# A fused two-layer transformer kernel: a new opening of the first phase (constant products ahead of the data, a first slab in two pieces on two queues, loads in order of use, squares of the rows later)

## The chip, the cores and the metric

The kernel runs on one core of one Trainium2 chip, as one program with one launch. The metric is the device time of that program in microseconds (us). The core has a matrix engine (TensorE, PE in the profile), whose weight loads are listed apart as PEld, a vector engine (DVE), a scalar engine (ACT), a general engine (POOL) and a queue engine (SP) that issues DMAs. Each engine works through a queue of its own in order, so an instruction that waits holds back all that stands behind it on that engine. Data comes from DRAM by DMA into the on-chip memory of 128 partitions; the matrix engine writes into eight accumulator banks of 128x512 numbers, which ACT and DVE empty.

## What is computed

Two transformer layers over 256 tokens of 2048 features. Layer 0 mixes tokens with two kinds of attention (block attention with 8 heads, and a compressed, selected and windowed attention with 8 heads in 2 groups), layer 1 with retention; each is followed by cross attention to a memory of 256 rows and a gated feed-forward net with a short convolution. All that the change touches lies at the start of layer 0:

```python
def _rmsnorm(x, g):
    y = xf * lax.rsqrt(jnp.mean(jnp.square(xf), axis=-1, keepdims=True) + RMS_EPS)
    return (y * g).astype(x.dtype)
...
hn = _rmsnorm(h, norm_mix[l])
mq, mk, mv, nq, nkc, nvc, nks, nvs, nkw, nvw, ng = _split(h @ w_in, AB_SIZES)
...
kc = _compress(k_c, pe_k, w1_k, w2_k)        # nkc -> compressed keys
vc = _compress(v_c, pe_v, w1_v, w2_v)        # nvc -> compressed values
p_c = softmax(q . kc);  o_c = p_c @ vc
o = gates[..., 0:1] * o_c + gates[..., 1:2] * o_s + gates[..., 2:3] * o_w
```

The first products of the kernel are nkc and nvc, 256 columns each, from columns 4096 to 4607 of `w_in_ab`. The kernel multiplies the weights with x times the gain first and applies the factor of the norm (one number per token, from the squares of the rows) to the results afterwards.

## The kernel before, in words

**Slabs and pieces.** The 2048 features are cut into 16 slabs of 128. A weight or an activation is kept as two parts, a high one (`hi`, an ACT copy to the rounded type fp32r) and a low one (`lo`, a DVE subtraction), and a product is the sum of three part products. `product_b_steps` (L258) makes 256 output columns with the weights as the stationary operand: per slab four matmuls of 512 columns (`upper`, L272: high weights on both parts of x) and four of 256 (`lower`, L277), counted over the two accumulators j of both first products. Every other step does `lower` first. `product_a_steps` (L295) makes columns with x as the stationary operand (L303 to L305). The two first products need all four accumulator pieces of the tag `acc` (L101); the product after them, columns 4864 to 5119, gets its two accumulators when those of the first of the two have been emptied by `halves` (L320): an ACT copy (L322), then a DVE addition (L324).

**The first phase (L359 to L409)** is written out by hand for ACT, DVE and PE (`manual_schedule`), so that their queues have the order of the code. It goes over 8 pairs of slabs p. For each pair SP issues the load of x (`load_x`) and of the two weight pieces (L388); ACT makes the high part of x (L197) and of the weights (L401), DVE the low parts (L200, L402); then each of the two products in `first` does one step. For pairs 0 to 3 the loads are pieces of 256 KB in order of use; then come all four remaining x loads, and weight loads of 512 KB for two pairs each. After pair 3, six tiny DVE memsets (L409) are placed on tiles which POOL's loads (constants, parameters, positions; L417, L421, L431, L453 and L128) fill later: POOL's loads wait for them.

**After the first phase** `layers()` (L1040) runs with only PE's order by hand; ACT, DVE, POOL and SP get theirs from the scheduler of the framework when the program is built. Beside the products stands a list of generators, `side`; `pump` (L244) advances the first two of them at each step of a product. Before the change the list is: `start_steps` (L619: loads of the rows, their squares on ACT by `norm.add`, L148, two steps after each load; then the norm's factors `col` and `row`; then, inside it, `angle_steps` for the rotary angles), `setup_steps`, and `compress` for k; `compress` for v is appended later. `compress` waits 8 steps, loads its weights and runs small matmuls (L687), ending for v with L723, which reads `hs` made by DVE at L716. `nsa_group` (L763) makes the scores against the compressed keys (L773), waits three steps and transposes the result (L803); DVE copies it to `pct` (L805). `nsa_head` (L808) then uses `pct` at L822, the first of the five matmuls that make a head's output.

Of the kernel before, what the change touches and what calls it, by code (L numbers as in the profile page):

```python
# [75 lines left out]
def hybrid_kernel(ctx: ExitStack, tc: tile.TileContext, a, out):  # L76
# [33 lines left out]

    ident = new([P, P])
    make_identity(nc, ident)
    ones = new([P, P])
    pool.memset(ones, 1.0)
# [143 lines left out]
    def product_b_steps(ws, xs, evac, step=4, n=None, turn=True):  # L258
# [4 lines left out]
        for i, k0 in enumerate(range(0, n, step)):  # L263
            ks = range(k0, min(k0 + step, n))
            parts = [next(ws) for _ in ks]
            last = ks[-1] == n - 1
            kj = [(k, j) for k in ks for j in range(2)]
            jk = [(k, j) for j in range(2) for k in ks]

            def upper(order, end):  # L270
                for k, j in order:
                    pe.matmul(acc[j], parts[k - k0][0][:, j * P : (j + 1) * P], xs[k], start=(k == 0),  # L272
                              stop=(end and k == n - 1))

            def lower(order, end):
                for k, j in order:
                    pe.matmul(acc[j][:, 0:S], parts[k - k0][1][:, j * P : (j + 1) * P], xs[k][:, 0:S], start=False,  # L277
                              stop=(end and k == n - 1))

            if turn and i % 2:  # L280
# [55 lines left out]
    def feed(norm, xs, gains):  # L336
# [12 lines left out]
        def f(g):  # L349
            for t in range(2):  # L350
# [9 lines left out]
    held = [[], []]  # L360
    ready = [deque(), deque()]
    first = [product_b_steps(iter(ready[i].popleft, None), xs_mix, lambda j, acc, i=i: held[i].append(halves(acc)),
                             step=2, n=ND) for i in range(2)]
    cst, cmask, tri_f, posi = new([P, 4]), new([P, 2, 16]), work((P, P)), new([P, S], I32, "w", 12)

    def load_x(p):

        nc.sync.dma_start(x_in[p].rearrange("p s t -> p (s t)"), a["x"][:, 2 * p * S : (2 * p + 2) * S])
# [5 lines left out]
    with tc.manual_schedule(engines=engines):  # L374
        act.activation(new([P, 1]), eps, AF.Copy, scale=eps)
        load_par(nc.sync, "mix")
        for p in range(ND // 2):
            i, c = p // 2, slice(p % 2 * 512, p % 2 * 512 + 512)
            if p % 2 == 0:
                raws = [raw_tile() for _ in range(2)]  # L380
                his = [new([P, 1024], F32R, "whi", 4) for _ in range(2)]
                los = [new([P, 1024], F32R, "wlo", 4) for _ in range(2)]
            if p < 4:
                load_x(p)
            for q in range(2):
                if p < 4 or p % 2 == 0:
                    d = c if p < 4 else slice(0, 1024)
                    nc.sync.dma_start(raws[q][:, d], w_ab.part(4 * i, 4, 4096 + 256 * q, 256)[:, d])  # L388
            if p == 3:
                for x in range(4, 8):  # L390
                    load_x(x)
            for s in (2 * p, 2 * p + 1):
                xs_mix.append(slab_tile())
                xhat_hi(xs_mix[s], x_in[p][:, s % 2, :], gain("mix")[:, s : s + 1])
            if p == 0:
                dve.tensor_copy(his[0][:, c], raws[0][:, c])
            for s in (2 * p, 2 * p + 1):
                xhat_lo(xs_mix[s], x_in[p][:, s % 2, :], gain("mix")[:, s : s + 1])
            for q in range(2):
                if p or q:  # L400
                    act.activation(his[q][:, c], raws[q][:, c], AF.Copy)  # L401
                dve.tensor_sub(los[q][:, c], raws[q][:, c], his[q][:, c].bitcast(F32))  # L402
# [3 lines left out]
            if p == 3:  # L406
# [205 lines left out]
    def mixer_ab(xs, row, col, kcv):  # L612
# [6 lines left out]
        def start_steps():  # L619
            norm = Norm()  # L620
            tg = [(t, g) for g in range(4) for t in range(2)]
            for i in range(10):
                if i < 8:
                    load_rows(*tg[i])
                if i > 1:
                    norm.add(*tg[i - 2])
                if i < 9:
                    yield
# [8 lines left out]
            yield from angle_steps(0, posi)  # L637
# [19 lines left out]
        def compress(i, kind, t, done):  # L657

            for _ in range(8):
# [79 lines left out]
        side.extend((start_steps(), setup_steps()))  # L739
# [23 lines left out]
        def nsa_group(g, qr, qu):  # L763
# [34 lines left out]
            yield  # L798
            yield
            yield  # L800
# [7 lines left out]
        def nsa_head(g, r, q):  # L808
# [9 lines left out]
            while len(comp) < 2:  # L818
# [389 lines left out]
```

## Time and profile before

| | before |
|---|---|
| time, median of 3 runs | 2839.22 us (2838.47 to 2839.59) |
| profiled execution, its own time | 2837.16 us |
| its span, first to last instruction | 2835.4 us (1.76 us lie around it) |
| PE busy | 2815.4 us (99%) |
| DVE busy | 1926.7 us (68%) |
| ACT busy | 1483.8 us (52%) |
| mean granted PE clock | 0.999 |

All engine times below are microseconds from the first instruction of the profiled execution. A timeline row has the start, the duration, the engine, the source line, the operation, output and inputs with their shapes, the count of merged instructions, and in brackets how long the engine had been idle before it and what released it. Matmuls overlap, and the end of one is modelled, so the pace of PE is read from start to start. A matmul between full float32 operands stands as two records in the trace.

### The profile page before, as it was taken

The numbers are of one execution on the slowest core, as the hardware profiler recorded it, in microseconds if no ns is written. First come the engines' busy times: TensorE is split into PE (matmuls) and PEld (weight loads), VectorE is DVE, ScalarE is ACT, GpSimd is POOL, SyncE is SP. The second block draws the span as 40 slices with busy tenths as digits, with TensorE's granted clock in tenths as the row PEclk, the third lists the DMA queues.
The fourth block names the chain that finished last, engine by engine and source line by source line (L and its number), as shares of the span: only waits on it lengthen the run. The fifth ranks groups of instructions, "written<-read, shape, count | busy, mean of one in ns | idle before, by whom it ended". The sixth has DMA issues, their size and how long they took to land.

```text
span 2835.4 us, 39564 instructions
## 1 busy us (share of the span) xinstructions
PE 2815.4 (99%) x14726; PEld 2404.8 (85%) x14726; DVE 1926.7 (68%) x3147; ACT 1483.8 (52%) x2193; POOL 29.9 (1%) x211
## 2 busy tenths in 40 slices
PE   8999999999999999999999999999999999999998
PEld 8888888888888888888888888888888888888887
DVE  7765766776767677665555555556777767676766
ACT  6444455664545555454444444444665645454554
POOL 0000000000000000000000000000000000000000
PEclk9999999999999999999999999999999999999999
DMA  9535564555555555555555555565545555555554
GB/s 320 163 120 162 182 209 170 173 191 193 186 193 188 191 193 203 191 185 179 179 179 178 193 178 179 183 206 190 186 168 189 189 191 191 191 188 193 192 188 155
DMA packets 150545, 530.12 MB, mean 187 GB/s; under 512 B 17040, under 2 KB 17456, under 8 KB 150352
## 3 DMA queue, kind: packets, MB, share of 16 engines
q1 hardware_dynamic: 148752, 523.65, 53.8%
q0 software_dynamic: 1024, 2.90, 0.4%
q8 instruction: 115, 1.88, 0.3%
q10 hardware_dynamic: 576, 1.05, 0.1%
q14 instruction: 78, 0.64, 0.1%
HBM read 525.43 MB, written 2.10 MB: 186 GB/s over the span
## 4 chain that ended last, share of the span: by engine, by line
PE 98%; DMA 1%; DVE 0%; ACT 0%; issue 0%; SPq 0%; ACTq 0%; DVEq 0%
PE acc L272 33%; PE acc L277 17%; PE acc L303 14%; PE acc L305 14%; PE acc L304 14%; PE bank L346 1%; PE bank L981 0%; DMA t<-in_w_in_ab_dram 0%; PE bank L499 0%; PE bank L491 0%; PE bank L479 0%; PE bank L1004 0%; PE bank L574 0%; PE bank L584 0%; PE bank L970 0%; PE bank L983 0%
## 5 line engine op out<-in xcount | busy, mean ns | idle before, releaser
L233 DVE TENSOR_TENSOR t<-t,t 128x1024 fp32r<-128x1024 f32 x954 | 1163.9, 1221 | 704.0 <-ACT t L232 701.1
L232 ACT ACTIVATE t<-t 128x1024 fp32r<-128x1024 f32 x954 | 1009.9, 1059 | 952.5 <-PE acc L305 564.2
L272 PE MATMUL acc<-t,t 128*128 128x512 f32 x4096 | 992.8, 392 | 6.6 <-DVE t L200 6.6
L272 PEld LDWEIGHTS acc<-t,t 128*128 128x128 f32 x4096 | 750.9, 189 | 151.6 <-DVE t L200 6.6
L303 PE MATMUL acc<-t,t 128*128 128x512 f32 (+2 forms) x1824 | 712.8, 391 | 2.6 <-DVE t L324 2.6
L305 PE MATMUL acc<-t,t 128*128 128x512 f32 (+2 forms) x1824 | 704.7, 386 | 0.0
L304 PE MATMUL acc<-t,t 128*128 128x512 f32 (+2 forms) x1824 | 704.1, 386 | 0.0
L277 PEld LDWEIGHTS acc<-t,t 128*128 128x128 f32 x4096 | 528.3, 191 | 22.2 <-issue 0.4
L277 PE MATMUL acc<-t,t 128*128 128x256 f32 x4096 | 539.4, 283 | 0.0
L303 PEld LDWEIGHTS acc<-t,t 128*128 128x128 f32 x1824 | 343.4, 188 | 72.4 <-DVE t L324 3.0
L304 PEld LDWEIGHTS acc<-t,t 128*128 128x128 f32 x1824 | 343.6, 188 | 69.0 <-issue 1.9
L305 PEld LDWEIGHTS acc<-t,t 128*128 128x128 f32 x1824 | 343.2, 188 | 69.3
L878 ACT ACTIVATE t<-acc 128x256 f32<-128x256 f32 x176 | 65.6, 373 | 151.1 <-PE acc L272 151.1
L881 DVE TENSOR_TENSOR t<-acc,t 128x256 f32<-128x256 f32 x176 | 74.1, 421 | 78.0 <-ACT t L878 77.8
L884 ACT ACTIVATE t<-t,t 128x256 f32<-128x256 f32 x176 | 104.6, 594 | 32.3 <-DVE t L882 32.0
L602 DVE TENSOR_TENSOR t<-t,acc 128x512 f32<-128x512 f32 x148 | 95.0, 680 | 2.1 <-PE acc L1099 2.1
L886 DVE SCALAR_TENSOR_TENSOR t<-t,t,t 128x256 f32<-128x256 f32 x176 | 84.5, 480 | 3.1
L885 DVE SCALAR_TENSOR_TENSOR t<-t,t,t 128x256 f32<-128x256 f32 x176 | 84.1, 478 | 0.7 <-ACT t L884 0.7
L882 DVE TENSOR_TENSOR t<-t,t 128x256 f32<-128x256 f32 x176 | 74.2, 422 | 3.0
L322 ACT ACTIVATE t<-acc 128x256 f32<-128x256 f32 x80 | 30.4, 382 | 67.0 <-PE acc L272 67.0
L324 DVE TENSOR_TENSOR t<-acc,t 128x256 f32<-128x256 f32 x80 | 33.4, 419 | 27.2 <-ACT t L322 27.0
L898 ACT ACTIVATE t<-t 128x256 f32<-128x256 f32 x88 | 36.0, 410 | 24.9 <-DVE t L886 24.9
(218 smaller groups left out, 1128.4 us busy)
## 6 DMA issues: line engine op xcount, KB each, us to landing
t<-in_w_up_dram SPq DMA_DIRECT2D x352, 512.0 KB, 3.3
t<-in_w_in_c_dram SPq DMA_DIRECT2D x192, 512.0 KB, 3.4
t<-in_w_down_dram SPq DMA_DIRECT2D x176, 512.0 KB, 3.3
t<-in_w_in_ab_dram SPq DMA_DIRECT2D x80, 512.0 KB, 3.6
t<-in_w_out_c_dram SPq DMA_DIRECT2D x64, 512.0 KB, 3.4
t<-in_w_out_ab_dram SPq DMA_DIRECT2D x32, 512.0 KB, 3.9
t<-in_w_kv_x_dram SPq DMA_DIRECT2D x32, 512.0 KB, 3.4
t<-in_w_q_x_dram SPq DMA_DIRECT2D x16, 512.0 KB, 3.2
```

The source lines that it names most:

```text
L232: act.activation(hi[:, 0 : m * ncol], raw[:, 0 : m * ncol], AF.Copy)
L233: dve.tensor_sub(lo[:, 0 : m * ncol], raw[:, 0 : m * ncol], hi[:, 0 : m * ncol].bitcast(F32))
L272: pe.matmul(acc[j], parts[k - k0][0][:, j * P : (j + 1) * P], xs[k], start=(k == 0), stop=(end and k == n - 1))
L277: pe.matmul(acc[j][:, 0:S], parts[k - k0][1][:, j * P : (j + 1) * P], xs[k][:, 0:S], start=False, stop=(end and k == n - 1))
L303: pe.matmul(o, xh, hi, start=(k == 0), stop=False)
L304: pe.matmul(o, xh, lo, start=False, stop=False)
L305: pe.matmul(o, xl, hi, start=False, stop=(k == n - 1))
L602: dve.tensor_add(part(t, g), part(t, g), acc)
L882: dve.tensor_mul(u[:, 2:], t, norm.r)
L884: act.activation(c, u[:, 2:], AF.Identity, bias=cp[:, 3, j : j + 1], scale=cp[:, 2, j : j + 1])
L885: dve.scalar_tensor_tensor(c, u[:, 1 : S + 1], cp[:, 1, j : j + 1], c, op0=ALU.mult, op1=ALU.add)
L886: dve.scalar_tensor_tensor(c, u[:, 0:S], cp[:, 0, j : j + 1], c, op0=ALU.mult, op1=ALU.add)
```

## The change

It makes the following edits; the line numbers of L375 and after are those of the kernel after the change.

1. POOL sets the tile `ones` first, before the identity. PE multiplies `ones` with itself 8 times (L379, 128x128 in float32) into a spare bank `warm`, before it needs any data.
2. The steps of the first products are `SPANS`: slab 0 alone, slab 1 alone, then pairs, so 9 steps and not 8, with the same matmuls in all. x and the weights of slabs 0 and 1 come in pieces of 128 KB; the two weight pieces of slab 0 are issued on ACT's queue, all else on SP's. The load of the gains (`par`) stands behind the first x piece.
3. All loads are issued in order of use, and all weight pieces after slab 1 have 256 KB. For slabs 8 to 13 they land in tiles of the tag `p`.
4. The six DVE memsets that POOL's loads wait for come after slabs 12 and 13 and not after slabs 6 and 7.
5. `start_steps` begins its row loads one step later, and squares a row piece 4 steps after its load and not 2.
6. `angle_steps` is a generator of its own behind `setup_steps` in `side`; `compress` waits 2 steps and not 8 after it is reached; `nsa_group` waits 6 steps and not 3 before its transposes; `nsa_head` waits also until `pct` of its group is there.

```diff
+    ones = new([P, P])
+    pool.memset(ones, 1.0)
     ident = new([P, P])
     make_identity(nc, ident)
-    ones = new([P, P])
-    pool.memset(ones, 1.0)
...
+    SPANS = [range(0, 1), range(1, 2)] + [range(k, k + 2) for k in range(2, ND, 2)]
...
-        act.activation(new([P, 1]), eps, AF.Copy, scale=eps)
-        load_par(nc.sync, "mix")
-        for p in range(ND // 2):
...
+        warm = bank()
+        for _ in range(8):
+            pe.matmul(warm[:, 0:P], ones, ones, start=True, stop=True)
+        raws = [None, None]
+        for ks in SPANS:
...
+            if ks[0] in (0, 4, 14):
+                raws = [raw_tile() for _ in range(2)]
+            elif ks[0] in (8, 10, 12):
+                raws = [new([P, 512], F32, "p", 7) for _ in range(2)]
+            load_x(ks[0], ks[0] + m)
             for q in range(2):
...
+                (nc.sync if ks[0] else nc.scalar).dma_start(raws[q][:, d], w_ab.part(ks[0] // 4 * 4, 4, 4096 + 256 * q, 256)[:, c])
+            if ks[0] == 0:
+                load_par(nc.sync, "mix")
+                act.activation(new([P, 1]), eps, AF.Copy, scale=eps)
...
-            if p == 3:
+            if p == 6:
...
-            for i in range(10):
-                if i < 8:
-                    load_rows(*tg[i])
-                if i > 1:
-                    norm.add(*tg[i - 2])
-                if i < 9:
-                    yield
+            for i in range(13):
+                if 0 < i < 9:
+                    load_rows(*tg[i - 1])
+                if i > 4:
+                    norm.add(*tg[i - 5])
+                yield
...
-            yield from angle_steps(0, posi)
...
-            for _ in range(8):
+            for _ in range(2):
                 yield
...
-        side.extend((start_steps(), setup_steps()))
+        side.extend((start_steps(), setup_steps(), angle_steps(0, posi)))
...
-            yield
-            yield
-            yield
+            for _ in range(6):
+                yield
...
-            while len(comp) < 2:
+            while len(comp) < 2 or g not in pcts:
```

Two places show what this moves. The first is the end of the first products, on ACT and DVE. On ACT, L148 is a square of a row piece, L322 the copy that empties an accumulator of the first products, L232 the high part of the next weights. Before:

```order
L148 ACTIVATE t_464,t_408<-t_74 128x512
L148 ACTIVATE t_485,t_408<-t_73 128x512
L232 ACTIVATE t_391<-t_390 128x1024
L148 ACTIVATE t_500,t_408<-t_74 128x512
L232 ACTIVATE t_431<-t_430 128x1024
L148 ACTIVATE t_521,t_408<-t_73 128x512
L148 ACTIVATE t_538,t_408<-t_74 128x512
L322 ACTIVATE t_346<-acc_111 128x256
L322 ACTIVATE t_350<-acc_112 128x256
```

After, in the same place (L408 is now the high part of the last first-phase weights):

```order
L408 ACTIVATE t_307<-t_348 128x512
L232 ACTIVATE t_415<-t_414 128x1024
L148 ACTIVATE t_528,t_432<-t_73 128x512
L322 ACTIVATE t_370<-acc_117 128x256
L232 ACTIVATE t_454<-t_453 128x1024
L322 ACTIVATE t_374<-acc_118 128x256
L148 ACTIVATE t_552,t_432<-t_74 128x512
L148 ACTIVATE t_575,t_432<-t_73 128x512
```

Before, six squares stand ahead of the first copy; after, one. The second weight conversion now stands between the two copies.

DVE in the same place, after the change: L425 makes a mask from a tile that POOL loads, L233 is the low part of the next weights (tiles 455 and 416), L324 the addition that frees an accumulator:

```order
L409 TENSOR_TENSOR t_309<-t_348,t_307 128x512
L425 CAST t_399<-t_85 128x128
L233 TENSOR_TENSOR t_416<-t_414,t_415 128x1024
L324 TENSOR_TENSOR t_372<-acc_117,t_370 128x256
L233 TENSOR_TENSOR t_455<-t_453,t_454 128x1024
L324 TENSOR_TENSOR t_376<-acc_118,t_374 128x256
```

Before, the like rows read (L418 is that cast):

```order
L418 CAST t_375<-t_85 128x128
L402 TENSOR_TENSOR t_299<-t_295,t_297 128x512
L200 SCALAR_TENSOR_TENSOR t_328<-t_82,t_72,t_328 128x256
L200 SCALAR_TENSOR_TENSOR t_330<-t_82,t_72,t_330 128x256
L402 TENSOR_TENSOR t_298<-t_294,t_296 128x512
L402 TENSOR_TENSOR t_299<-t_295,t_297 128x512
L233 TENSOR_TENSOR t_392<-t_390,t_391 128x1024
L233 TENSOR_TENSOR t_432<-t_430,t_431 128x1024
L324 TENSOR_TENSOR t_348<-acc_111,t_346 128x256
```

The cast has moved behind the last work of the first phase, and the low part of the second weights stands ahead of the second addition in both.

The second place is PE in the first 512-column product after the four query blocks. Before, two matmuls of `compress` for v (L723) stand there; the transposes for `pct` (L803) stood some 70 matmuls earlier:

```order
L304 MATMUL acc_1643<-t_1670,t_136 128x512
L305 MATMUL acc_1643<-t_1669,t_136 128x512
L723 MATMUL bank_1686<-t_1316,t_1628 128x128
L723 MATMUL bank_1690<-t_1316,t_1634 128x128
L479 MATMUL bank_1694<-t_61,t_1566 128x128 x3
```

After, the transposes (L807) and the matmul that reads `pct` (L826, tile 1704) stand side by side:

```order
L304 MATMUL acc_1682<-t_1685,t_132 128x512
L305 MATMUL acc_1682<-t_1684,t_132 128x512
L807 MATMUL bank_1701<-t_63,t_1448 128x128 x2
L826 MATMUL bank_1706<-t_1704,t_1513 128x256
L506 MATMUL bank_1706<-t_1625,t_407 128x256
```

DVE copies the transposes to `pct`. Before, the copy (L805) stands among weight conversions:

```order
L233 TENSOR_TENSOR t_1580<-t_1578,t_1579 128x1024
L652 TENSOR_TENSOR t_1445<-t_1445,t_1446 32x256
L233 TENSOR_TENSOR t_1646<-t_1644,t_1645 128x1024
L805 COPY t_1518<-bank_1515 128x256
L233 TENSOR_TENSOR t_1670<-t_1668,t_1669 128x1024
```

After, DVE has there, behind the first addition (L324) of the last query block, whose accumulators are 1519 and 1520:

```order
L760 TENSOR_TENSOR t_1653<-t_1651,t_405 128x256
L654 STREAM_SHUFFLE t_1656<-t_1651 32x256
L655 TENSOR_TENSOR t_1655<-t_1651,t_404 128x256
L656 SCALAR_TENSOR_TENSOR t_1656<-t_1656,t_406 32x256
L233 TENSOR_TENSOR t_1821<-t_1819,t_1820 128x1024
L657 TENSOR_TENSOR t_1655<-t_1655,t_1656 32x256
L324 TENSOR_TENSOR t_1663<-acc_1520,t_1661 128x256
L760 TENSOR_TENSOR t_1665<-t_1663,t_405 128x256
L654 STREAM_SHUFFLE t_1668<-t_1663 32x256
L655 TENSOR_TENSOR t_1667<-t_1663,t_404 128x256
L656 SCALAR_TENSOR_TENSOR t_1668<-t_1668,t_406 32x256
L809 COPY t_1704<-bank_1701 128x256
```

That addition and eleven more rows stand ahead of the copy (L809). L728, the new line of L723, now stands in the middle of the query blocks. From the 1552nd row of PE on, and from like places on the other engines, the order of both kernels is the same to the end.

More of the change, by code (lines that the diff above doesn't have):

```diff
@@ L256, in run, with product_b_steps @@
                 pump(n)
-    def product_b_steps(ws, xs, evac, step=4, n=None, turn=True):
+    def product_b_steps(ws, xs, evac, groups=None, n=None):
         acc = acc_tile()
         n = n or len(xs)
-        for i, k0 in enumerate(range(0, n, step)):
-            ks = range(k0, min(k0 + step, n))
+        for i, ks in enumerate(groups or [range(k, min(k + 4, n)) for k in range(0, n, 4)]):
+            k0 = ks[0]
             parts = [next(ws) for _ in ks]
@@ L278, in lower @@
                               stop=(end and k == n - 1))
-            if turn and i % 2:
+            if i % 2:
                 lower(kj, False)
@@ L360, in hybrid_kernel, with load_x @@
     held = [[], []]
+    SPANS = [range(0, 1), range(1, 2)] + [range(k, k + 2) for k in range(2, ND, 2)]
     ready = [deque(), deque()]
     first = [product_b_steps(iter(ready[i].popleft, None), xs_mix, lambda j, acc, i=i: held[i].append(halves(acc)),
-                             step=2, n=ND) for i in range(2)]
+                             groups=SPANS, n=ND) for i in range(2)]
     cst, cmask, tri_f, posi = new([P, 4]), new([P, 2, 16]), work((P, P)), new([P, S], I32, "w", 12)
-    def load_x(p):
-        nc.sync.dma_start(x_in[p].rearrange("p s t -> p (s t)"), a["x"][:, 2 * p * S : (2 * p + 2) * S])
+    def load_x(s0, s1):
+        nc.sync.dma_start(x_in[s0 // 2][:, s0 % 2 : s0 % 2 + s1 - s0, :].rearrange("p s t -> p (s t)"),
+                          a["x"][:, s0 * S : s1 * S])
     def load_rows(t, g):
@@ L374, in hybrid_kernel @@
     with tc.manual_schedule(engines=engines):
[L375 to L380 removed]
+        warm = bank()
[3 more added lines that the diff above has]
+        for ks in SPANS:
+            p, m = ks[0] // 2, len(ks)
+            c = slice(ks[0] % 4 * 256, ks[0] % 4 * 256 + 256 * m)
+            if ks[0] % 4 == 0:
                 his = [new([P, 1024], F32R, "whi", 4) for _ in range(2)]
                 los = [new([P, 1024], F32R, "wlo", 4) for _ in range(2)]
[L383 to L392 removed]
+            if ks[0] in (0, 4, 14):
+                raws = [raw_tile() for _ in range(2)]
+            elif ks[0] in (8, 10, 12):
+                raws = [new([P, 512], F32, "p", 7) for _ in range(2)]
+            d = slice(0, 512) if ks[0] in (8, 10, 12) else c
+            load_x(ks[0], ks[0] + m)
+            for q in range(2):
+                (nc.sync if ks[0] else nc.scalar).dma_start(raws[q][:, d], w_ab.part(ks[0] // 4 * 4, 4, 4096 + 256 * q, 256)[:, c])
+            if ks[0] == 0:
+                load_par(nc.sync, "mix")
+                act.activation(new([P, 1]), eps, AF.Copy, scale=eps)
+            for s in ks:
                 xs_mix.append(slab_tile())
@@ L395, in hybrid_kernel @@
             if p == 0:
-                dve.tensor_copy(his[0][:, c], raws[0][:, c])
-            for s in (2 * p, 2 * p + 1):
+                dve.tensor_copy(his[0][:, c], raws[0][:, d])
+            for s in ks:
                 xhat_lo(xs_mix[s], x_in[p][:, s % 2, :], gain("mix")[:, s : s + 1])
```

5 lines of the change are left out of this document (2 added, 3 removed).

## The prediction

> **What bounds the kernel now.** I read the page first (span, busy shares, chain), then who PE waits for, then PE's timeline where those waits lie, and the engines that end them.
>
> ```profile
> span 2835.4 us, 39564 instructions
> PE 2815.4 (99%) x14726; PEld 2404.8 (85%) x14726; DVE 1926.7 (68%) x3147; ACT 1483.8 (52%) x2193; POOL 29.9 (1%) x211
> PE 98%; DMA 1%; DVE 0%; ACT 0%; issue 0%; SPq 0%; ACTq 0%; DVEq 0%
> ```
>
> PE is the bound: 98% of the chain that ended last. So the change is worth what it takes off PE's waits and off the time in which PE runs slower than it can. All waits of PE are three:
>
> ```profile
> PE acc L272 <- DVE t L200: 6.6, 1, 6.6
> PE acc L303 <- DVE t L324: 2.6, 1, 2.6
> PE bank L723 <- DVE t L716: 1.7, 1, 1.7
> ```
>
> The first is the start, the second the end of the first products, the third lies at 143 us. PE's timeline of the first phase (start, duration, line, count):
>
> ```profile
> 6.56 2.07 PE L272 MATMUL acc<-t,t 128*128 128x512 f32 x4 [6.56 <-DVE t L200]
> 8.44 1.05 PE L277 MATMUL acc<-t,t 128*128 128x256 f32 x4
> ...
> 13.42 2.02 PE L272 MATMUL acc<-t,t 128*128 128x512 f32 x8
> ...
> 19.04 2.02 PE L272 MATMUL acc<-t,t 128*128 128x512 f32 x8
> 20.89 0.63 PE L277 MATMUL acc<-t,t 128*128 128x256 f32 x4
> 21.36 1.09 PE L272 MATMUL acc<-t,t 128*128 128x512 f32 x4
> ...
> 30.26 1.09 PE L272 MATMUL acc<-t,t 128*128 128x512 f32 x4
> 33.91 0.39 PE L303 MATMUL acc<-t,t 128*128 128x256 f32 x1 [2.55 <-DVE t L324]
> ...
> 35.09 0.41 PE L303 MATMUL acc<-t,t 128*128 128x256 f32 x1
> ...
> 38.29 0.36 PE L303 MATMUL acc<-t,t 128*128 128x256 f32 x1
> ...
> 38.49 0.28 PE L304 MATMUL acc<-t,t 128*128 128x256 f32 x1
> ```
>
> Two pairs of slabs take 19.04 - 13.42 = 5.62 us, so **a pair costs 2.81 us** at PE's full pace. The first four matmuls took 8.44 - 6.56 = 1.88 us, twice their later 0.93 (20.89 - 19.04 is 1.85 for eight): PE ran at half its clock at the start. The first products end at 30.26 + 1.09 = 31.35. Behind the wait of 2.55 us, 15 matmuls from 35.09 to 38.29 go at 0.213 us each, where four L277 of the same width take 21.36 - 20.89 = 0.47, so 0.118 each: 15 x 0.095 and the transition make **1.5 us lost to a lower clock**. The stretch view has it as the granted clock (columns: stretch, its length, busy of PE, PEld, DVE, ACT, POOL, then PEclk, DMA share, GB/s):
>
> ```profile
> 35.00:40.00 5.00, 5.00 (x32) 5.00 (x31) 4.19 (x11) 3.23 (x7) 0.00 (x0) 0.66 0.90 301
> 140.00:160.00 20.00, 18.30 (x96) 14.52 (x95) 14.14 (x46) 9.19 (x23) 0.00 (x0) 1.00 0.37 118
> ```
>
> So an idle of 2.55 us was followed by a drop, the idle of 1.7 us in the second row by none. The Trainium skill (TensorE: Matmul & The Clock Gate, Why this matters for your kernels) puts the limit at idle gaps of about 3 us; by that, 2.55 us would have cost no clock, term 3 below would be nothing, and the sum 4.5 us and not 6.0. The trace decides: it did cost.
>
> **Term 1, the start: 31.35 becomes 28.2.** The data of the first pairs arrive on ACT and DVE like this:
>
> ```profile
> 1.18 0.42 SPq L368 DMA_DIRECT2D t<-in_x_dram  x1
> 4.67 0.91 ACT L197 ACTIVATE t<-t,t 128x256 fp32r<-128x256 f32 x2 [2.35 <-DMA t<-in_x_dram]
> 8.40 1.16 ACT L401 ACTIVATE t<-t 128x512 fp32r<-128x512 f32 x2
> 11.06 1.29 DVE L402 TENSOR_TENSOR t<-t,t 128x512 fp32r<-128x512 f32 x2
> ```
>
> x, issued at 1.18, was there at 4.67. It now goes first, at 0.74, with half the bytes, the weights beside it on ACT's queue. From issue to use took 3.5 us for 256 KB; I take 2.9 for 128 KB, so 3.65, and with one L197 (half of 0.91) and one low part (as long) PE's first real matmul is at about 4.75. Two steps of one slab (1.4 each) end at 7.55. Slabs 2 and 3 then wait for data: their first high weights were ready at 8.40 + 0.58, all loads now run 1.18 - 0.74 = 0.44 earlier with the same bytes ahead of them, so PE goes on at 8.55. That step ends at 11.36. Slabs 4 and 5 begin with low parts, which were ready at 11.06 + 0.65, now at 11.27, just in time. From 8.55 on PE is the limit: seven pairs, 8.55 + 7 x 2.81 = 28.2. **Saved: 3.15 us.** If the loads gain nothing it ends at 28.65; if short pieces cost another 0.5 us, at 29.1; if slabs 2 and 3 came without a wait, at 27.2.
>
> The 8 constant products are 16 records, as two such products (two of 128 columns, in the chain) are 4:
>
> ```profile
> 51.78 0.44 PE bank L193 x4
> ```
>
> That is 0.11 us a record at the full clock; at half of it, 0.213, the 16 take 3.4 us, from about 1.1 (`ones` is set first on POOL) to 4.5. They cost nothing, since PE has no other work until 4.75; what they can change is the clock. Were it still low in the two single steps, those would end at 4.75 + 5.6 = 10.35, not 7.55: 1.8 us lost past 8.55, and the end at 30.0.
>
> **Term 2, the wait of 2.55 becomes 1.15.** Why it was 2.55 is on ACT:
>
> ```profile
> 31.74 0.63 ACT L148 ACTIVATE t<-t 128x512 f32<-128x512 f32 x1 [0.25 <-DMA t<-in_rows_dram]
> ...
> 33.03 0.64 ACT L322 ACTIVATE t<-acc 128x256 f32<-128x256 f32 x2
> 33.56 1.06 ACT L232 ACTIVATE t<-t 128x1024 fp32r<-128x1024 f32 x1
> ```
>
> The copies stood behind squares that waited for rows. Now one square stands ahead, long done. The first of the two products ends 1.4 us before 28.2; its first accumulator is ready at 26.6, the copy (0.38) ends at 27.0. But the next weight conversion (1.06) stands between the copies, to 28.05, and on DVE its low part stands ahead of the second addition:
>
> ```profile
> 31.52 1.23 DVE L233 TENSOR_TENSOR t<-t,t 128x1024 fp32r<-128x1024 f32 x1 [1.57 <-ACT t L232]
> 35.79 0.42 DVE L324 TENSOR_TENSOR t<-acc,t 128x256 f32<-128x256 f32 x1
> ```
>
> 28.1 + 1.15 (1.23 less overlap) + 0.42 = 29.65, and PE goes on at 29.7. Three matmuls on the first accumulator (0.35) run from 28.2, so PE idles 1.15. **Saved: 1.4 us.** Bounds: 0.3, if the addition needn't stand behind the weights, and the old 2.55.
>
> **Term 3, the slow stretch: gone.** 1.15 us is less than the 1.7 that brought no drop. **Saved: 1.5 us.**
>
> **Term 4, the wait at L723 goes, one at the new L826 comes.** `hs` is now made in the middle of the query blocks, with 70 matmuls between it and its reader; I count its 1.7 us as gone. But `pct` is now read right behind its transposes, and its copy stands behind the two evacuations of the last query block. Their pace on DVE, and PE at the start and after twelve matmuls of the 512-column product:
>
> ```profile
> 124.33 0.41 DVE L324 TENSOR_TENSOR t<-acc,t 128x256 f32<-128x256 f32 x1
> ...
> 126.33 1.21 DVE L233 TENSOR_TENSOR t<-t,t 128x1024 fp32r<-128x1024 f32 x1
> 127.47 0.41 DVE L652 TENSOR_TENSOR t<-t,t 32x256 f32<-32x256 f32 x1
> ```
> ```profile
> 130.04 0.42 DVE L805 COPY t<-bank 128x256 f32<-128x256 f32 x1 [1.03 <-PE bank L803]
> 137.11 0.42 DVE L324 TENSOR_TENSOR t<-acc,t 128x256 f32<-128x256 f32 x1
> 137.40 0.39 PE L303 MATMUL acc<-t,t 128*128 128x512 f32 x1
> 140.13 0.49 PE L479 MATMUL bank<-t,t 128*128 128x128 f32 x3
> 140.38 0.47 PE L303 MATMUL acc<-t,t 128*128 128x512 f32 x1
> ```
>
> Six 256-column operations take 126.33 - 124.33 = 2.0 us, 0.333 each, the weights 1.14. Let E be the end of the last query block. The first addition starts 0.29 before E (137.11 against 137.40); five short operations, the weights and six more make 1.67 + 1.14 + 2.0 = 4.8, so the copy starts at E + 4.5 and `pct` is there at E + 5.0. PE has until then three transposes (140.38 - 140.13 = 0.25), twelve matmuls (140.13 - 137.40 = 2.73) and two more transposes (0.25): E + 3.25. **PE waits 1.75: cost against L723, 0.05 us.** At least it is 0.6 (drain and copy alone); with DVE two microseconds behind, 3.75, and then the clock drops as well (1.5).
>
> Other moved steps lie beside PE: the angles now run on DVE between weights that PE needs 2 us later or more; later squares delay `col`, which PE reads 22 us after 29.7.
>
> **The sum.** 3.15 + 1.4 + 1.5 - 0.05 = 6.0 us off the profiled 2837.16 (span 2835.4). The median of the runs lies 2.06 above the profiled execution; I take the difference from it: 2839.2 - 6.0 = **2833.2**. A measurement of this kernel can tell about 0.2% from no change, 5.7 us, so faster begins at 2833.5: the forecast lies right at that line.
>
> **Rivals.**
> - *Better: PE starts earlier and `pct` comes sooner* (first products end at 27.2, wait of 0.6): 1.0 + 1.15 more, a gain of 8.2, 2831.0. For it: DVE has idle time ahead of the last query block.
> - *`pct` late:* DVE 2 us behind, wait of 3.75 and a drop: 3.5 less, gain 2.5, 2836.7. For it: weight conversions stand close there.
> - *The constant products do not do what they are for:* the clock is low until about 8 us. The first products end at 30.0: gain 4.2, 2835.0. The Trainium skill (TensorE: Matmul & The Clock Gate, Part 1: The HAM clock gate) says that the clock is judged in windows of 3.4 us that run free, so that a burst of 3.4 us can straddle two. Where the windows lie, no row of before can tell.
> - *Slower: the mask tile.* The cast L425 now stands on DVE ahead of everything that frees PE at 28.2, and its load is issued by POOL after the memsets moved behind slabs 12 and 13.
>
> ```profile
> 14.71 0.67 POOL L453 DMA_DIRECT2D t<-in_c_cols_dram  x1 [12.99 <-DVE t L409]
> t<-in_c_tri_dram POOLq DMA_DIRECT2D x1, 64.0 KB, 5.5
> DMA to landing us min/median/max: 5.5/6.3/10.8
> ```
>
> These slabs need buffers that PE frees at 8.55 + 3 x 2.81 = 17.0; with two conversions the memsets come at 18.3, the mask's issue, third on POOL, at 19.5, and its landing (5.5 us) at 25.0. For PE to go on at 29.7, cast, two weight conversions and two additions must follow it (0.2 + 2 x 1.15 + 0.35 + 0.45 = 3.3): needed is 26.4. Each us past that costs one, and from about one us late the drop of 1.5 comes back. Slower than before it is from a landing at 30.9, 11.4 us after the issue, and by 0.2% from 36.6, 17 us; at 17.5 us the time is 37.0 - 26.4 + 1.5 - 6.0 = 6.1 above, 2845.3. For it: the slowest row load (last line, longest value) took 10.8 us. Against it: the mask's own 5.5.
>
> **Chances.** Forecast 0.50 (on either side of the line, 0.30 to 0.20), better 0.22, `pct` late 0.14, cold start 0.10, mask late 0.04. Faster 0.30 + 0.22 + 0.02 (a cold start with a short wait at L826) = 0.54; same 0.20 + 0.14 + 0.08 + 0.01 (mask a little late) = 0.43; slower 0.03. The range, 2829.8 to 2836.9, goes from a little beyond the better case to the late `pct`; it holds the bounds of the terms one at a time and leaves out the mask and sums of several.
>
> **What will show it.** Right: 16 records ahead of a first L272 near 4.8 at 0.23 us each; the first L303 near 28.2 with some 1.15 us idle behind it; clock 1.00 at 30 to 40 us; no wait at L728, one near 1.75 us at L826 on DVE L809. Wrong: L272 at 0.43 us after 5 us, a clock below 1 after L826, a first L303 past 29.5, or a wait of DVE at L425.

## The result, and the profile after

The changed kernel takes 2873.82 us (2873.65 to 2874.09) against 2839.2 us: 34.6 us slower, ratio 1.0125, 95% interval 1.0113 to 1.0136. The forecast was 2833.2, the upper end of the range 2836.9. Yet the page and the waits of PE after the change look like the forecast:

```profile
span 2872.0 us, 39614 instructions
PE 2857.9 (100%) x14742; PEld 2395.6 (83%) x14742; DVE 1928.0 (67%) x3150; ACT 1485.3 (52%) x2194; POOL 29.9 (1%) x211
```
```profile
PE bank L826 <- DVE t L809: 1.8, 1, 1.8
PE acc L303 <- DVE t L324: 1.0, 1, 1.0
PE bank L379 <- POOL t L112: 1.0, 1, 1.0
PE acc L272 <- DVE t L200: 0.9, 2, 0.6
```

PE waited 10.9 us before and waits 4.7 now: 6.2 less. But its busy time went from 2815.4 to 2857.9, 42.5 more, for 16 more matmul records. 42.5 - 6.2 = 36.3 is the whole difference of the spans (36.6). PE does the same work more slowly, and the clock isn't it: the mean granted clock is 0.999 in both. The groups of PE, different shapes apart (busy us, mean ns of one), first of before, then of after:

```profile
L272 PE MATMUL acc<-t,t 128*128 128x512 f32 x4096 | 992.8, 392 | 6.6 <-DVE t L200 6.6
L303 PE MATMUL acc<-t,t 128*128 128x512 f32 x1760 | 693.5, 394 | 0.0
L305 PE MATMUL acc<-t,t 128*128 128x512 f32 x1760 | 685.7, 390 | 0.0
L304 PE MATMUL acc<-t,t 128*128 128x512 f32 x1760 | 685.0, 389 | 0.0
L277 PE MATMUL acc<-t,t 128*128 128x256 f32 x4096 | 539.4, 283 | 0.0
```
```profile
L272 PE MATMUL acc<-t,t 128*128 128x512 f32 x4096 | 1010.2, 396 | 0.9 <-DVE t L200 0.9
L303 PE MATMUL acc<-t,t 128*128 128x512 f32 x1760 | 704.6, 400 | 0.0
L305 PE MATMUL acc<-t,t 128*128 128x512 f32 x1760 | 696.4, 396 | 0.0
L304 PE MATMUL acc<-t,t 128*128 128x512 f32 x1760 | 696.3, 396 | 0.0
L277 PE MATMUL acc<-t,t 128*128 128x256 f32 x4096 | 529.3, 280 | 0.1
```

Every group of 512-column matmuls costs 10.7 to 17.4 us more, that of 256 columns 10.1 less, 40.4 in sum, in the same numbers of matmuls. PE's timeline inside a 512-column product, far behind everything that the diff reorders (before, then after), shows it per matmul:

```profile
1499.69 0.39 PE L303 MATMUL acc<-t,t 128*128 128x512 f32 x1
...
1503.77 0.39 PE L303 MATMUL acc<-t,t 128*128 128x512 f32 x1
```
```profile
1500.63 0.40 PE L303 MATMUL acc<-t,t 128*128 128x512 f32 x1
...
1503.43 0.40 PE L303 MATMUL acc<-t,t 128*128 128x512 f32 x1
```

Before, 18 matmuls start in 4.08 us, one every 227 ns; after, 12 in 2.80 us, one every 233 ns. This time from start to start is called the pitch below. No line, wait or engine of the profile explains it; PE isn't waiting. What the built program shows, and no view of the profile, is where the tiles lie (bytes in a partition of the on-chip memory, SBUF; numbers of the accumulator banks, PSUM):

```
                              before    after
weight tiles (hi, lo, raw)     68896    68864   first one
slabs of x                    118048   118048   first one
accumulators                  0 to 3   4 to 7   PSUM banks
```

Tiles get their place in the order in which names are first asked for. The diff moves `act.activation(new([P, 1]), ...)` from ahead of the loop into its first turn, behind the weight tiles, so its 32 bytes of scratch no longer lie below them: the block of the weight tiles starts 32 bytes further down, the slabs stay. Inside the block the order changes too, from raw, hi, lo to hi, lo, raw; but each of these tiles has 4096 bytes and each slab 2048, so modulo 256 bytes all weight tiles start at 32 before and at 0 after, and all slabs at 32 in both. And `warm = bank()` is now the first PSUM tile, which swaps the accumulators' banks with the others.

The first phase itself, in PE's timeline after:

```profile
1.00 3.78 PE L379 MATMUL bank<-t 128*128 128x128 f32 x16 [1.00 <-POOL t L112]
5.04 1.22 PE L272 MATMUL acc<-t,t 128*128 128x512 f32 x2 [0.27 <-DVE t L200]
...
9.44 1.20 PE L272 MATMUL acc<-t,t 128*128 128x512 f32 x4 [0.62 <-DVE t L200]
...
29.04 0.63 PE L277 MATMUL acc<-t,t 128*128 128x256 f32 x4
29.51 0.28 PE L303 MATMUL acc<-t,t 128*128 128x256 f32 x1
...
31.05 0.38 PE L303 MATMUL acc<-t,t 128*128 128x256 f32 x1 [1.03 <-DVE t L324]
```

It ends earlier than before (29.04 + 0.63 = 29.67 against 31.35), as forecast in kind if not in size.

### The profile page after: what moved, and what is told of

Same layout as the page of the kernel before. It is cut to its first block, busy times and chain, and to the rows that moved or that the text cites. A ratio compares the mean times of both kernels' runs of the same rounds, so it can differ in the third digit from the quotient of the medians.

```text
span 2872.0 us, 39614 instructions
## 1 busy us (share of the span) xinstructions
PE 2857.9 (100%) x14742; PEld 2395.6 (83%) x14742; DVE 1928.0 (67%) x3150; ACT 1485.3 (52%) x2194; POOL 29.9 (1%) x211
## 4 chain that ended last, share of the span: by engine, by line
PE 99%; DVE 0%; ACT 0%; DMA 0%; issue 0%; SPq 0%
PE acc L272 33%; PE acc L277 17%; PE acc L303 15%; PE acc L305 15%; PE acc L304 15%; PE bank L346 1%; PE bank L985 0%; PE bank L506 0%; PE bank L498 0%; PE bank L486 0%; PE bank L1008 0%; PE bank L591 0%; PE bank L581 0%; PE bank L974 0%; PE bank L987 0%; PE bank L496 0%
## 5 line engine op out<-in xcount | busy, mean ns | idle before, releaser
L233 DVE TENSOR_TENSOR t<-t,t 128x1024 fp32r<-128x1024 f32 x954 | 1163.5, 1221 | 730.2 <-ACT t L232 723.9
L232 ACT ACTIVATE t<-t 128x1024 fp32r<-128x1024 f32 x954 | 1009.6, 1059 | 993.2 <-PE acc L305 594.8
L272 PE MATMUL acc<-t,t 128*128 128x512 f32 x4096 | 1010.2, 396 | 0.9 <-DVE t L200 0.9
L272 PEld LDWEIGHTS acc<-t,t 128*128 128x128 f32 x4096 | 747.0, 188 | 163.4 <-ACT t L408 1.1
L303 PE MATMUL acc<-t,t 128*128 128x512 f32 (+2 forms) x1824 | 723.1, 396 | 1.0 <-DVE t L324 1.0
L305 PE MATMUL acc<-t,t 128*128 128x512 f32 (+2 forms) x1824 | 714.7, 392 | 0.0
L304 PE MATMUL acc<-t,t 128*128 128x512 f32 (+2 forms) x1824 | 714.6, 392 | 0.0
L277 PEld LDWEIGHTS acc<-t,t 128*128 128x128 f32 x4096 | 518.8, 188 | 26.0 <-issue 0.6
L277 PE MATMUL acc<-t,t 128*128 128x256 f32 x4096 | 529.3, 280 | 0.1
L303 PEld LDWEIGHTS acc<-t,t 128*128 128x128 f32 x1824 | 343.2, 188 | 81.1 <-issue 1.9
L305 PEld LDWEIGHTS acc<-t,t 128*128 128x128 f32 x1824 | 342.9, 188 | 79.9
L322 ACT ACTIVATE t<-acc 128x256 f32<-128x256 f32 x80 | 30.5, 383 | 74.5 <-PE acc L272 72.4
L324 DVE TENSOR_TENSOR t<-acc,t 128x256 f32<-128x256 f32 x80 | 33.4, 419 | 29.9 <-ACT t L322 29.7
L200 DVE SCALAR_TENSOR_TENSOR t<-bank,t,t 128x256 fp32r<-128x256 f32 x112 | 47.0, 475 | 1.4 <-ACT t L197 1.4
```

Source lines behind the costliest of these rows:

```text
L232: act.activation(hi[:, 0 : m * ncol], raw[:, 0 : m * ncol], AF.Copy)
L233: dve.tensor_sub(lo[:, 0 : m * ncol], raw[:, 0 : m * ncol], hi[:, 0 : m * ncol].bitcast(F32))
L303: pe.matmul(o, xh, hi, start=(k == 0), stop=False)
L304: pe.matmul(o, xh, lo, start=False, stop=False)
L305: pe.matmul(o, xl, hi, start=False, stop=(k == n - 1))
```

## The experiments

**1. Which of the two moves: the weights' address or the banks?** Four kernels, each with one thing put back or brought in. The changed kernel with its weights at 68896 again:

```diff
+        scrap = new([P, 1])
         raws = [None, None]
...
-                act.activation(new([P, 1]), eps, AF.Copy, scale=eps)
+                act.activation(scrap, eps, AF.Copy, scale=eps)
```

> In the changed kernel the 512-column matmuls start every 233 ns in place of every 227, in all stages alike, and the change also moved memory: all weight tiles 32 bytes down (68864 in place of 68896) and the accumulators from PSUM banks 0-3 to 4-7. This is the changed kernel with the weight tiles back at 68896 (one column of scratch is allocated ahead of them) and nothing else. Theory weights' address: the pitch is 227 ns again and the time some 2833 us, what the first phase was forecast to gain below 2839.2. Theory PSUM banks: nothing changes, 2873.8. Theory of order (the pitch follows from how the stream began, not from addresses): 2873.8 as well.

Measured: 2834.46 us (2832.04 to 2836.38) beside 2837.79 of the kernel before on the same chip, ratio 0.9990 (0.9980 to 0.9999). The groups are those of before again, to the digit of the mean:

```profile
L272 PE MATMUL acc<-t,t 128*128 128x512 f32 x4096 | 991.3, 392 | 0.9 <-DVE t L200 0.9
L303 PE MATMUL acc<-t,t 128*128 128x512 f32 x1760 | 693.6, 394 | 0.0
L277 PE MATMUL acc<-t,t 128*128 128x256 f32 x4096 | 540.2, 283 | 0.1
```

The changed kernel with its accumulators back in banks 0 to 3:

```diff
+        for _ in range(2):
+            acc_tile()
         warm = bank()
```

> The changed kernel with the accumulators back in PSUM banks 0-3 (four unused ones are allocated ahead of the warm-up's bank) and the weights left at 68864. Theory PSUM banks: 512-column pitch 227 ns and some 2833 us. Theory weights' address, and theory of order: 2873.8, pitch 233.

Measured: 2873.43 us, ratio 1.0123 (1.0107 to 1.0140): nothing changed. The kernel before with its weights at 68864:

```diff
-        act.activation(new([P, 1]), eps, AF.Copy, scale=eps)
-        load_par(nc.sync, "mix")
         for p in range(ND // 2):
+            if p == 0:
+                first_raws = [raw_tile() for _ in range(2)]
+                his = [new([P, 1024], F32R, "whi", 4) for _ in range(2)]
+                los = [new([P, 1024], F32R, "wlo", 4) for _ in range(2)]
+                act.activation(new([P, 1]), eps, AF.Copy, scale=eps)
+                load_par(nc.sync, "mix")
...
-            if p % 2 == 0:
+            if p == 0:
+                raws = first_raws
+            elif p % 2 == 0:
```

> The kernel before with its weight tiles at 68864 as in the changed kernel (its column of scratch is allocated behind them), accumulators left in banks 0-3. Theory weights' address: pitch 233 ns and about 2839.2 + 40 = 2879 us (the 34.6 measured and the some 6 that the first phase should gain). Theory PSUM banks, and theory of order: 2839.2.

Measured: 2878.04 us, ratio 1.0141 (1.0126 to 1.0156). The kernel before, with nothing of the change but 32 bytes, is 40 us slower than itself. Two of its groups:

```profile
L272 PE MATMUL acc<-t,t 128*128 128x512 f32 x4096 | 1010.7, 396 | 6.5 <-DVE t L200 6.5
L303 PE MATMUL acc<-t,t 128*128 128x512 f32 x1760 | 704.1, 400 | 0.0
```

And the kernel before with its accumulators in banks 4 to 7 (one unused `bank()` ahead of all):

> The kernel before with its accumulators in PSUM banks 4-7 as in the changed kernel (one unused bank is allocated first), weights left at 68896. Theory PSUM banks: pitch 233 ns and about 2879 us. Theory weights' address, and theory of order: 2839.2.

Measured: 2838.45 us, ratio 1.0000 (0.9990 to 1.0009). So the weights' address is the cause, shown in both directions, and the banks and the order of the work have no part in it. Nor has the order of the tiles in the block: the first of these kernels is fast with the new order, the third slow with the old one.

**2. The address itself, or its distance from the slabs?** The same changed kernel with the scratch column made wider, or put ahead of the weights, or padded, so that weights and slabs start elsewhere. First both at multiples of 128 (a scratch of 32 columns ahead of the weights):

> So far: weight tiles at 32 above a multiple of 64 bytes and slabs at 32 above one gave a 512-column pitch of 227 ns, weights at a multiple of 64 and slabs at 32 above one 233 ns. Here, in the changed kernel, weights and slabs both start at multiples of 128 (68992 and 118144). Theory relative: PE reads stationary and moving rows at once, and the pitch is 227 when both start at the same place within 64 bytes; then 227 here, 2834 us. Theory absolute: weight rows at a multiple of 64 are the slow ones whatever the slabs do; then 233 here, 2874 us. Third outcome: rows that start on whole 64 bytes are read best when both do, and the pitch falls below 227, the time by over 30 us below 2834.

Measured: 2833.21 us, ratio 0.9982 (0.9973 to 0.9991). Both at 64 above a multiple of 128 (a scratch of 16 columns ahead of the weights):

> Weights and slabs both at 64 above a multiple of 128 (68928 and 118080). Relative: 227 ns, 2834 us. Absolute, if it goes by 64 bytes: 233 ns, 2874; if only a multiple of 128 is slow: 227, 2834. The same as weights and slabs both at multiples of 128 if only 64 bytes matter.

Measured: 2833.71 us, 0.9985 (0.9975 to 0.9994). Weights as in the kernel before, slabs 32 further (one column of scratch ahead of the weights, another behind them):

> Weights at 32 above a multiple of 64 as in the kernel before (68896), slabs at a multiple of 64 (118080). Relative: 233 ns, 2874 us. Absolute: 227 ns, 2834 us.

Measured: 2875.85 us, 1.0133 (1.0116 to 1.0150). Weights as in the changed kernel, slabs 32 further (16 columns behind the weights):

> Weights at a multiple of 128 (68864) as in the changed kernel, slabs 32 bytes further up than there, at 64 above a multiple of 128 (118080). Relative within 64 bytes: 227 ns, 2834 us; relative within 128 bytes: 233 ns, 2874. Absolute: 233 ns, 2874.

Measured: 2855.13 us, 1.0059 (1.0044 to 1.0074), between the two. So it is the distance and no absolute address: both moved together cost nothing, the slabs alone cost as much as the weights alone.

**3. By what rule?** Only the width of the scratch behind the weights varies from here on, a column for every 4 bytes: for distance 96 the edit is

```diff
-                act.activation(new([P, 1]), eps, AF.Copy, scale=eps)
+                act.activation(new([P, 24])[:, 0:1], eps, AF.Copy, scale=eps)
```

> Weights at a multiple of 128 bytes, slabs 96 above one (68864 and 118112). The difference of the two starts, taken within 128, has given 512-column pitches of 227 ns at 0 (three placements) and 233 at 32 (two), and at 64 229 where slabs move and 233 where weights move. Theory: the pitch is a function of the difference modulo 128, and 96 is 32 the other way round: 233 ns, about 2873 us. Rival: only rows that start ahead of the others by 32 are hit, then 96 is as good as 0 or as 64: 2833 to 2855.

Measured: 2891.58 us, 1.0190 (1.0176 to 1.0204). Neither theory: 96 is worse than 32.

> Weights at a multiple of 128, slabs 128 bytes further up than in the changed kernel's grid of equal starts (68864 and 118144: the difference is 0 modulo 128, not modulo 256 or 512 as it was in all the fast kernels). Theory modulo 128: 227 ns, 2833 us. Rival, modulo 256 or 512: some other pitch, above 227 (2850 or more) or below it.

Measured: 2876.78 us, 1.0138 (1.0124 to 1.0151). The theory of a rule modulo 128 falls.

> Distance from the start of the weight tiles to that of the slabs: 256 bytes modulo 512 (68864 and 118272). Measured so far: 0 gives 2833, 32 2873 to 2876, 64 2855, 96 2892, 128 2877 us. Modulo 256: 2833, pitch 227. Modulo 512: another pitch, 2850 to 2895.

Measured: 2833.39 us, 0.9983 (0.9973 to 0.9992): modulo 256.

> Distance 384, that is -128 modulo 512 (68864 and 118400). A rule modulo 256 makes it equal to 128: 2877. A rule modulo 512 that treats both sides alike: 2877 too. One that goes by which of the two reads lies ahead: another time.

Measured: 2876.74 us, 1.0137 (1.0121 to 1.0153), as 128: modulo 256 again.

> Distance 448, -64 modulo 512 (68864 and 118464). Both sides alike: 2855, as 64. By which read is ahead: another time.

Measured: 2840.27 us, 1.0007 (0.9997 to 1.0017), and 64 gave 2855: the two sides are not alike.

> Distance 480, -32 modulo 512 (68864 and 118496). Both sides alike: 2873, as 32. By which read is ahead: another time, and if it is below 2833 (pitch below 227), this is the better placement.

Measured: 2879.67 us, 1.0147 (1.0131 to 1.0163): no better placement, and about as slow as 32.

> Distance 160 modulo 256 (68864 and 118176), the one step of 32 bytes not yet measured. So far 0 gives 2833, 32 2873, 64 2855, 96 2892, 128 2877, 192 2840 and 224 2880 us. Theory: only 0, where both rows start at the same place of 256 bytes, has the steady pitch of 227 ns; 160 lies in the range of the others, 2840 to 2892. Rival: it is below 2833, and then the kernel before doesn't have the best placement either.

Measured: 2884.32 us, 1.0164 (1.0147 to 1.0181). All together, with the mean time from the start of one matmul to the start of the next in long stretches of one kind, read from the trace (the first matmuls of a stretch left out):

| slabs' start minus weights', modulo 256 bytes | time, us | 512 columns, weights move (L303 to L305), ns | 512 columns, slabs move (L272) | 256 columns (L277) |
|---|---|---|---|---|
| 0 (before; four of the runs above) | 2833.2 to 2834.5 | 226.7 | 226.7 | 120.0 |
| 32 (the changed kernel; three runs) | 2873.4 to 2878.0 | 233.3 | 233.4 | 116.7 |
| 64 | 2855.1 | 233.3 | 229.0 | 115.8 |
| 96 | 2891.6 | 234.3 | 233.4 | 119.9 |
| 128 (two runs) | 2876.8, 2876.7 | 233.0 | 233.2 | 118.7 |
| 160 | 2884.3 | 233.4 | 234.5 | 118.7 |
| 192 | 2840.3 | 228.9 | 233.3 | 113.3 |
| 224 | 2879.7 | 233.3 | 233.3 | 118.4 |

The times of row 0 are those of the changed kernel with its weights or slabs moved; the upper end of row 32, 2878.0, is the kernel before with its weights moved. The rule is modulo 256; within it there is no order that these runs explain. Zero is the best of the eight for the 512-column matmuls, and with 96 the worst for those of 256 columns, of which there is less.

**4. PE's own reads, or any tile against any other?** The low parts of the weights moved, to distance 224, the high parts at 0 (the raw tiles behind the low parts, which these matmuls don't read, stand at 224 too):

```diff
+        scrap = new([P, 1])
         raws = [None, None]
...
+                if ks[0] == 0:
+                    new([P, 1])
                 los = [new([P, 1024], F32R, "wlo", 4) for _ in range(2)]
...
-                act.activation(new([P, 1]), eps, AF.Copy, scale=eps)
+                new([P, 56])
+                act.activation(scrap, eps, AF.Copy, scale=eps)
```

> High parts of the weights at distance 0 modulo 256 from the slabs (68896 and 118304), low parts at 224, as at distance 480 (85312). Theory: a matmul's pitch goes by the rows that PE itself reads for it and for the weight load beside it. Then the product with weights as stationary operand keeps 227 ns in its high part (distance 480 had 233, 18 us in all), its low part goes like that of distance 480 (117 to 120 ns), and of the three matmuls of the other product, where weights move, those around the low part go slower (11 to 21 of 32 us): 2841 to 2851 us. Rival: what counts is any pair of tiles that is in use at once, by whatever engine: 2880, all at 233. Third: the low parts don't matter, 2833.

Measured: 2861.36 us, ratio 1.0085 (1.0068 to 1.0102): above the 2841 to 2851 of the theory, below the 2880 of its rival. Its groups, and L272 with all weight tiles at distance 224 (480):

```profile
L272 PE MATMUL acc<-t,t 128*128 128x512 f32 x4096 | 997.8, 393 | 1.1 <-ACT t L412 0.8 <-DVE t L200 0.3
L303 PE MATMUL acc<-t,t 128*128 128x512 f32 x1760 | 702.2, 399 | 0.0
L304 PE MATMUL acc<-t,t 128*128 128x512 f32 x1760 | 698.1, 397 | 0.0
L305 PE MATMUL acc<-t,t 128*128 128x512 f32 x1760 | 690.3, 392 | 0.0
```
```profile
L272 PE MATMUL acc<-t,t 128*128 128x512 f32 x4096 | 1009.5, 396 | 1.0 <-ACT t L408 0.8 <-DVE t L200 0.2
```

L272, which loads high parts alone, keeps most of its pace (997.8 against 991.3 at distance 0 and 1009.5 at 224): in a run of sixteen the starts are 224 to 236 ns apart on the mean for the first nine, then 227. At distance 0 it takes five to come to 227, and at 224 it never does (231 to 234). Where high and low parts alternate, all three lines go at 230 to 234 ns, not only the one that streams the low part (227 at distance 0, 233 at 224), and that is what the expectation had too low. The pitch of a matmul thus depends on the operands of PE's matmuls ahead of it too. Whether PE's reads of the stationary and of the moving rows get in each other's way is not shown: no run here separates these reads.

**5. Terms of the forecast, at distance 0.** The kernel of experiment 1 with `pct` made after three turns again, as before, in place of six:

```diff
-            for _ in range(6):
+            for _ in range(3):
                 yield
             b = bank()
```

> The changed kernel with its weights back at 68896, and three turns of waiting ahead of the transposes that make the first group's tile, as in the kernel before, in place of six: the tile is then made between two chunks of the last query block. Theory: the wait of 1.9 us on its copy is gone and nothing takes its place: 1.9 us below the same kernel with six turns (2834.5, span 2830.3), so span 2828.4. Rival: the transposes or their reader wait at the earlier place too, by up to 1.9: no gain.

Measured: 2830.61 us (2830.16 to 2832.45), ratio to before 0.9975 (0.9966 to 0.9984), span 2828.8 against 2830.3. PE's waits, then the stretches of five us around the place (length, busy of PE, PEld, DVE, ACT, POOL, PEclk, DMA share, GB/s):

```profile
PE bank L379 <- POOL t L112: 1.0, 1, 1.0
PE acc L303 <- DVE t L324: 0.8, 1, 0.8
PE acc L272 <- ACT t L409: 0.7, 1, 0.7
PE acc L272 <- DVE t L200: 0.6, 1, 0.6
PE acc L277 <- DVE t L410: 0.4, 1, 0.4
```
```profile
135.00:140.00 5.00, 5.00 (x24) 3.74 (x23) 4.97 (x18) 3.38 (x8) 0.00 (x0) 1.00 0.09 35
140.00:145.00 5.00, 5.00 (x31) 4.26 (x30) 2.62 (x5) 2.05 (x4) 0.00 (x0) 1.00 0.55 133
```

No wait on the copy is left, PE is busy throughout, and nothing took its place: in span 1.5 us are gained of the 1.9 expected. In the medians it is 3.9, more than the wait alone; that most executions of the kernel with six turns also had a clock drop behind the wait would fit (a mean clock of 0.998 in 8 of 10, against 1 of 10 here), but it isn't shown: the one trace of that kernel has no drop. This kernel is the fastest of all, 7.2 us below the kernel before. And the kernel of experiment 1 without the constant products:

```diff
-        warm = bank()
-        for _ in range(8):
-            pe.matmul(warm[:, 0:P], ones, ones, start=True, stop=True)
```

> The changed kernel with its weights back at 68896, without the eight products of the constant tile. Theory: the clock then rises some 4.6 us behind the first real matmul, as in the kernel before (6.56, 11.15), at about 9.5 in place of 5.8; the two single-slab steps, 2.8 us at full pace, take 4.5 more or less, 0.7 of it in what PE waits for slabs 2 and 3 anyway: first products end 1.5 us later, span 2831.8. Rival: PE waits for data there anyhow, no change, 2830.3.

Measured: 2834.55 us, ratio 0.9988 (0.9980 to 0.9997), with them 2834.46 and 0.9990: in time the same. In the trace its clock rises at 10.16 in place of 5.78, and PE's timeline has

```profile
5.44 1.22 PE L272 MATMUL acc<-t,t 128*128 128x512 f32 x2 [5.44 <-DVE t L200]
...
9.87 1.69 PE L272 MATMUL acc<-t,t 128*128 128x512 f32 x6
...
29.62 0.64 PE L277 MATMUL acc<-t,t 128*128 128x256 f32 x4
31.70 0.39 PE L303 MATMUL acc<-t,t 128*128 128x256 f32 x1 [1.44 <-DVE t L324]
```

where the kernel with them has

```profile
9.13 1.19 PE L272 MATMUL acc<-t,t 128*128 128x512 f32 x4 [0.73 <-DVE t L200]
...
11.56 1.50 PE L277 MATMUL acc<-t,t 128*128 128x256 f32 x8
...
28.76 0.64 PE L277 MATMUL acc<-t,t 128*128 128x256 f32 x4
29.98 0.39 PE L303 MATMUL acc<-t,t 128*128 128x256 f32 x1 [0.58 <-DVE t L324]
...
31.45 0.38 PE L303 MATMUL acc<-t,t 128*128 128x256 f32 x1 [0.85 <-DVE t L324]
```

The first products end at 30.26 and 29.40: 0.86 us are gained, not 1.5. Behind the additions the gain shrinks to 0.6 (31.70 against 31.45 less the three matmuls that are done by then, 0.36). Most of the rest of the spans' difference (2833.1 against 2830.3) is a clock drop at 140 us, which only the one without them had in its profile (below).

## Why the prediction was wrong, point by point

**The step that failed** is the first inference: "PE is the bound ... So the change is worth what it takes off PE's waits and off the time in which PE runs slower than it can." Whatever lay behind 145 us was taken as unchanged, since the instructions there are the same in the same order. They are, but their operands aren't where they were, and PE's time for one matmul depends on that. The 13,472 matmuls of the groups above cost 3.0 ns more each on the mean (40.4 us), and that outweighs every wait of the first phase. No rival held it; the slower one (the mask tile) was another mechanism. Three of the signs named for being wrong did show in the changed kernel (a wait of DVE at L425, the first L303 at 29.51, a clock below 1 behind L826), but together they stand for some three microseconds, not 34.6: the 0.9 by which the sum below falls short, and the clock drop, up to 1.9.

The terms, read from the changed kernel at distance 0 (experiment 1), where they can be seen alone:

- *Start: 31.35 to 28.2 forecast, 29.40 measured*, saved 1.95 and not 3.15. The first matmul came nearly as said (4.98, against 4.75). The single steps ended at 9.13 - 0.73 = 8.4: they took 3.4 us and not 2.8, most of the difference because the clock rose only at 5.78 (the first two L272 took 0.93 us up to the start of the next line, two later ones 0.46). Slabs 2 and 3 were later: PE went on at 9.13, not at 8.55. Seven pairs of 2.81 from there give 28.8; most of the rest is a stall in the third pair, where eight L277 took 1.50 us (row at 11.56 above; seven starts at 0.12 us and the last one's 0.28 make 1.12). PE's weight loads waited there for the low parts of slabs 4 and 5 (idle 0.34 us until 12.32, ended by DVE L410), which the forecast had just in time at 11.27.
- *Wait behind the first products: 1.15 forecast*, 0.58 + 0.85 = 1.43 measured, in two pieces, since both additions were late; 1.03 in the changed kernel. The mask's cast did stand in front of them.

```profile
27.53 0.23 DVE L425 CAST t<-t 128x128 bf16<-128x128 f32 x1 [3.21 <-DMA t<-in_c_tri_dram]
27.68 1.22 DVE L233 TENSOR_TENSOR t<-t,t 128x1024 fp32r<-128x1024 f32 x1
28.81 0.42 DVE L324 TENSOR_TENSOR t<-acc,t 128x256 f32<-128x256 f32 x1
```

  In the changed kernel DVE waited 3.21 us for the mask, until 27.53 and not 25.0, past the 26.4 named as the limit: its load landed 4.8 us after the issue, but POOL issued it at 22.7 and not at 19.5. PE still lost only 1.03 us: the second addition stood behind a weight conversion that was waiting for ACT anyway (L233 at 29.43). At distance 0 the mask came at 28.23, 1.8 us past the limit, and the two waits of PE are 0.3 us above the forecast, not 1.8.
- *Slow stretch at 35 us: gone*, as forecast.
- *`pct`: 1.75 forecast*, 1.79 measured in the changed kernel, 1.85 at distance 0, and no wait at L728. Right, by the count of DVE's operations. But that a wait of this size brings no drop, as the sum assumed, was wrong: in the changed kernel the clock fell.
- *Sum: 6.0 forecast*; the span at distance 0 is 2830.3 against 2835.4, 5.1 less. The terms as measured give 1.95 + 1.12 + 1.5 - 0.15 = 4.4 of it; where the other 0.7 come from is not traced. In times the four kernels at distance 0 lie 3.3 to 5.3 us below the kernel before, ratios 0.9982 to 0.9990. So the mechanism of the first phase was right, its gain was put somewhat too large, and the change would have been a small gain without the 32 bytes.

## What to carry to other kernels

When an edit adds, drops or moves the allocation of a tile, even a scratch column, compare the addresses of the tiles that the dominant matmuls read before reading anything else into the time; here it was forty microseconds against five. If PE is busy nearly all of the span, read the start-to-start time of a matmul in an undisturbed stretch of both traces: a change of pitch at equal clock was placement here, and neither waits nor the chain showed it. Fix the distance between stationary and moving tiles on purpose (here 0 modulo 256 bytes), so that later edits don't move it.

## What the runs showed of the hardware that was not expected

**The distance between PE's operands.** A 512-column matmul starts every 226.7 ns where weight tiles and slabs start at the same place modulo 256 bytes, and every 228.9 to 234.5 ns otherwise; in times 2833 to 2892 us for the same instructions. The Trainium skill (SBUF — State Buffer, SBUF: two separate sides) says that on the engines' side of the memory only the port pair that DVE and GpSimd share causes contention and that PE never waits on anyone; these runs don't show another engine in PE's way, but they do show that PE's own pace goes by where its operands lie.

**When the clock drops.** The wait for `pct` was 1.79 us in the changed kernel and 1.85 at distance 0, with a drop behind the shorter one only (stretches as above):

```profile
140.00:145.00 5.00, 5.00 (x19) 4.08 (x19) 0.43 (x1) 0.38 (x1) 0.00 (x0) 0.69 0.37 105
```
```profile
140.00:145.00 5.00, 5.00 (x29) 4.28 (x28) 0.95 (x4) 1.44 (x2) 0.00 (x0) 1.00 0.32 105
```

The kernel before with its banks swapped idles 2.5 us at the place where the kernel before idles 2.55, without a drop (a row of PE's waits, then a stretch):

```profile
PE acc L303 <- DVE t L324: 2.5, 1, 2.5
```

```profile
35.00:40.00 5.00, 5.00 (x44) 5.00 (x43) 5.00 (x14) 3.29 (x8) 0.00 (x0) 1.00 0.97 302
```

All changes of the clock in a trace lie a whole number of 3.41 us apart (after: up at 6.62, down at 139.74, which is 39 times that). Count the windows of 3.41 us from the rise: in the 20 traces, up to the last matmul, the clock fell behind a window in which PE idled 1.79 us or more in 12 of 13 cases, and never behind one with 1.70 or less. The 2.5 us without a drop fell across an edge, 0.9 and 1.6, and so did the 1.7 us of the kernel before by which the forecast judged (0.9 and 0.8). The one exception is the 1.85 of experiment 1, which ends 0.07 us ahead of the edge. The Trainium skill (TensorE: Matmul & The Clock Gate, Part 1: The HAM clock gate) has such windows of 3.4 us, running free, and the lower clock after one idle window. The traces agree on the windows, but with the one exception the drop came from about half a window of idle on (the limit lies between 1.70 and 1.79 us), not from a whole one. In span a drop cost 1.4 to 1.9 us here (2832.0 to 2832.2 with one against 2830.3 without, and 2835.4 against 2834.0 for the kernel before and the one with its banks swapped, all at distance 0); the other waits of these kernels differ a little too.
